# Last ConvFFN of a hybrid decoder step: weights kept over two parts, the last norm without GpSimd, Newton's steps by column

## The chip, the cores and the metric

The kernel runs on one core of a Trainium2 chip. The metric is the time of one execution on the device in microseconds (us). Engines in the profile: PE is TensorE's matrix products, PEld its weight loads, DVE is VectorE, ACT is ScalarE, POOL is GpSimd, SP is SyncE, which issues the DMAs here.

## The reference

One step of a two-layer decoder for a prompt group of 512 tokens and a sample group of 64 (8 sequences of 8 tokens); 576 tokens in all, model width 1024, all in fp32. Layer 0 is attention of two kinds, layer 1 a chunked gMLP. Behind each mixer stands a ConvFFN:

```python
def conv_ffn(h, prev, w_up, w_conv, b_conv, w_down):
    up = h @ w_up                                  # 1024 -> 2 * 2816
    full = jnp.concatenate([prev, up], axis=1)
    y = b_conv
    for k in range(CONV_W):                        # causal, per column, width 3
        y = y + w_conv[k] * full[:, k:k + T]
    gate, val = jnp.split(y, 2, axis=-1)
    return (gelu(gate) * val) @ w_down             # 2816 -> 1024
```

and around each of the four sub-layers `x = layer_norm(ALPHA * x + (1 + gate) * sublayer(h), g, b)`, where `h = x * (1 + scale) + shift` comes from a conditioning vector. The norm takes (x - mean) / sqrt(var + eps), times g, plus b. The last ConvFFN's norm gives the outputs `y_prompt` and `y_sample`.

## The kernel before

Activations lie transposed: 8 blocks of 128 model columns on the partitions, 576 tokens along the free axis. fp32 products are made of three reduced-precision ones: `split_to` (L757) and `weights` (L243) divide a tensor into a high half (a cast on ScalarE) and a low half (a subtraction), and `product` (L287) adds wh*h, wh*l and wl*h over the blocks of a chunk, in PSUM. The tokens come in two parts: part 0 is 0 to 255, part 1 is 256 to 575 (256 prompt tokens and the 64 of the samples). An execution order per engine is made by a planner, from a model of the engines, with the place in the program as priority; `high_priority(offset=n)` shifts that place, `late` ties an instruction behind the one before it on its engine.

`weights` loads a unit of 128 x 1024 by a DMA into a raw buffer, casts it into a high buffer and subtracts into a low one, three buffers of each (`WB`). Which engine subtracts goes by the letters of `lows` in turn: 'g' is GpSimd, 'v' VectorE; in the products that end in a norm it is `LB` = 'gv'.

`ffn` (L471) runs over 22 pairs of hidden blocks. For each it makes the up-projections of gate and value, the convolution (ScalarE and VectorE), the gelu and the split, and it calls the down-projection chunk by chunk (`CH`). The last two chunks, hidden blocks 14 to 17 and 18 to 21, go through `accumulate` (L306) with a norm: part 1 first, through both chunks and all 8 output blocks, then part 0. A unit holds two output blocks of a chunk, so there are four units per chunk and part, and each is loaded and converted for either part: 16 in all. Each block's product goes to `add_gated` (L434), which adds it to the residual on VectorE (L439; part 1 also L442 and L444 for the samples). There are four PSUM buffers for products.

In the second of the two chunks `Norm.collect` (L71) follows every second block: it transposes the residual to rows of tokens (L83, L91), takes statistics on VectorE (L86, L93) and copies the rows on ScalarE (L87, L94). `finish(part)` (L117) calls `moments` (L446): aggregation (L452), then the inverse root in three Newton steps of three small instructions each, on all columns at once (L460 to L462), a column for each 128 tokens: 3 in part 1, 2 in part 0; the gMLP's own norm has 5. For the last norm `prepare` (L96) loads g and b as rows, and `output` (L185) makes the result: for part 1 the normalisation on ScalarE (L195), times g on VectorE (L196), plus b on GpSimd (L197); for part 0 `centre` (L170) has already made (row - mean) * g before Newton's steps, one of its four pieces on VectorE (L180) and three on ScalarE and GpSimd (L182, L183), and one instruction on VectorE remains for each (L199). L200 sends each piece of 512 columns to the output. `finish(1)` stands before part 0's products in the program, and its instructions mix with them.

For the inner norms `finish` normalises the rows (L134, L136), transposes them back (L153) and makes the next stage's modulated input, whose high and low halves are the tiles `xh` and `xl` (made by `pair(xp, [P, KB, T], "x")`, one buffer each), which all up-projections read.

Of the kernel before, what the change touches and what calls it, by code (L numbers as in the profile page):

```python
# [10 lines left out]
F32 = mybir.dt.float32  # L11
# [3 lines left out]
OP = mybir.AluOpType  # L15
# [3 lines left out]
P = 128  # L19
# [30 lines left out]
TWB = 3  # L50
BP = 200
LOWS = 'g'
LA = 'g'
# [6 lines left out]
class Norm:  # L60
# [56 lines left out]
    def finish(self, part):  # L117
# [3 lines left out]
        if last:  # L121
            return self.output(part, r, None)
        shift = self.pool.tile([P, 2 + part], F32, name="shift", bufs=2)
        nc.vector.scalar_tensor_tensor(shift, mv[:, :, 0], -1.0, r, op0=OP.mult, op1=OP.mult)
        if not self.nxt:
            return self.output(part, r, shift)
        t0 = PARTS[part][0]
# [42 lines left out]
    def centre(self, mv):  # L170

        nc, rt = self.net.nc, self.rt
        low = self.pool.tile([P, 2], F32, name="low")
        nc.vector.tensor_scalar(low, mv[:, :, 0], -1.0, None, op0=OP.mult)
        for half in range(2):
            cols = slice(512 * half, 512 * half + 512)
            for i in range(2):
                row, g = rt[:, i, cols], self.gb[:, 0, cols]
                if half == i == 0:
                    nc.vector.scalar_tensor_tensor(row, row, mv[:, i, 0:1], g, op0=OP.subtract, op1=OP.mult)  # L180
                else:
                    nc.scalar.activation(row, row, AF.Identity, bias=low[:, i:i + 1])  # L182
                    nc.gpsimd.tensor_tensor(row, row, g, op=OP.mult)  # L183

    def output(self, part, r, shift):  # L185

        net, nc, rt = self.net, self.net.nc, self.rt
        for half in range(2):
            cols = slice(512 * half, 512 * half + 512)
            for i in range(2 + part):  # L190
# [3 lines left out]
                if part:  # L194
                    nc.scalar.activation(row, row, AF.Identity, bias=shift[:n, i:i + 1], scale=r[:n, i:i + 1])  # L195
                    nc.vector.tensor_tensor(row, row, g, op=OP.mult)  # L196
                    nc.gpsimd.tensor_tensor(row, row, b, op=OP.add)  # L197
                else:
                    nc.vector.scalar_tensor_tensor(row, row, r[:n, i:i + 1], b, op0=OP.mult, op1=OP.add)  # L199
                nc.sync.dma_start(net.a["o_y"][t0:t0 + n, cols], row)  # L200


class Net:
# [102 lines left out]
    def accumulate(self, x, src, chunks, g1, psum, pool, between=None, norm=None):  # L306


        ws = {}

        def step(k0, ops, ob, part):
            m = len(ops)

            n = 1024 // (m * P) if norm else 1
            key = k0, ob // n, part if norm else 0
            if key not in ws:
                cols = slice(k0 * P, (k0 + m) * P)
                unit = src[ob, :, cols] if n == 1 else src[ob:ob + n, :, cols].rearrange("o p k -> p o k")
                ws[key] = self.weights(unit, n * m * P)
            acc = self.product(psum, *ws[key][:2], ob % n * m, ops, part)  # L320
            self.add_gated(x, acc, g1, ob, pool, part)

        if norm is None:
# [6 lines left out]
            return  # L330
        keep, self.lows = self.lows, LB
        for part in (1, 0):
            for k0, ops in chunks:
                for ob in range(8):
                    step(k0, ops, ob, part)
                    if between:
                        between()
                    if k0 == chunks[-1][0]:
                        norm.collect(ob, part)
            if part:  # L340
                norm.prepare()
# [104 lines left out]
    def moments(self, stats, pool, then=None):  # L446
# [12 lines left out]
        for _ in range(3):  # L459
            nc.vector.tensor_mul(z, y, y)  # L460
            nc.vector.tensor_mul(z, z, v)  # L461
            nc.vector.scalar_tensor_tensor(y, z, 1.5, y, op0=OP.add, op1=OP.mult)  # L462
        return mv, y
# [1170 lines left out]
```

## Time and profile before

| | us |
|---|---|
| median of 3 runs | 1940.66 |
| lowest, highest | 1937.17, 1941.69 |
| the profiled execution | 1944.53 |
| its span | 1942.8 |
| mean granted clock of TensorE in it | 0.972 |

The profile is of one execution. The span goes from the first instruction to the end of the last; the rest of the execution's time lies around it. In a row of a timeline stand the start in us from the span's start, the time it took (of several in a row: from the first start to the last end), the engine, the line, the operation, the tiles it writes and reads, their shapes and the count; in square brackets the idle time before it and who ended it. A row of the chain of waits has start, length, engine, tile, line and count. A row of windows has a stretch and its length, then the busy time of PE, PEld, DVE, ACT and POOL with the count of their instructions, the granted clock of TensorE (1.00 is full, 0.50 the lower level), the share of the DMA engines and GB/s; for the instructions of one line alone only the engines that run it are listed. A row of groups has line, engine, operation, tiles, shapes and count, then the busy time, the mean duration of one in ns and the idle time before.

### The profile page before, as it was taken

What the parts mean: (1) busy time and instruction counts of PE and PEld (TensorE: products, weight loads), DVE (VectorE), ACT (ScalarE), POOL (GpSimd) and SP (SyncE); (2) the same over time, 40 slices, a digit from 0 to 9 for tenths busy, and PEclk for the clock granted to TensorE, in tenths of its full rate; (3) what the DMA queues carried; (4) which work ended last, traced back from release to release, by engine and by line L of the source; (5) the groups of instructions that cost most, each with busy time, mean ns of one, the idle gap of its engine ahead of it and who ended that gap; (6) DMA issues with size and microseconds to landing.
All of it is one profiled execution on the core that took longest, in us unless ns stands there. A gap on an engine that the chain in (4) does not pass through costs nothing. (4 is left out here: it accounts for less than half of the span.)

```text
span 1942.8 us, 37068 instructions
## 1 busy us (share of the span) xinstructions
PE 1826.5 (94%) x14460; PEld 1622.8 (84%) x14460; DVE 1157.8 (60%) x2426; ACT 743.7 (38%) x1382; POOL 351.3 (18%) x518
## 2 busy tenths in 40 slices
PE   6889999899889899999999999999998999999996
PEld 4647877655459799999999989999997999999995
DVE  2549963465448754545556963465577655555577
ACT  2323222255443542424345432422234535344543
POOL 2323511110015310101012330110013101010124
PEclk9989999999899999999999999999998999999997
DMA  8346577797874335353543422332132222213242
GB/s 288 127 155 219 179 253 244 241 307 232 266 240 149 116 131 189 135 161 135 195 141 107 131 92 78 97 97 59 63 112 72 78 97 67 97 56 108 87 139 92
DMA packets 140865, 283.36 MB, mean 146 GB/s; under 512 B 32722, under 2 KB 43922, under 8 KB 140690
## 3 DMA queue, kind: packets, MB, share of 16 engines
q1 hardware_dynamic: 139970, 278.64, 43.9%
q0 software_dynamic: 720, 2.36, 0.5%
q8 instruction: 114, 1.87, 0.4%
q14 instruction: 61, 0.50, 0.1%
HBM read 270.00 MB, written 10.94 MB: 145 GB/s over the span
## 5 line engine op out<-in xcount | busy, mean ns | idle before, releaser
L298 PE MATMUL acc<-xl,wh 128*128 128x256 f32 (+1 forms) x1664 | 496.2, 298 | 5.9 <-DVE xl L162 5.9
L298 PE MATMUL acc<-xh,wh 128*128 128x256 f32 (+1 forms) x1664 | 498.6, 300 | 2.9 <-ACT xh L161 1.7
L298 PE MATMUL acc<-xh,wl 128*128 128x256 f32 (+1 forms) x1664 | 495.0, 298 | 0.0
L251 ACT CAST wh<-wr 128x1024 fp32r<-128x1024 f32 (+2 forms) x276 | 260.7, 949 | 537.3 <-PE acc L298 375.3
L254 DVE TENSOR_TENSOR wl<-wr,wh 128x1024 fp32r<-128x1024 f32 (+2 forms) x211 | 226.7, 1076 | 248.0 <-ACT wh L251 222.4
L298 PEld LDWEIGHTS acc<-xh,wh 128*128 128x128 f32 x1664 | 318.2, 191 | 11.7 <-issue 6.4
L298 PEld LDWEIGHTS acc<-xl,wh 128*128 128x128 f32 x1664 | 318.5, 191 | 7.5 <-DVE xl L162 7.1
L298 PEld LDWEIGHTS acc<-xh,wl 128*128 128x128 f32 x1664 | 318.5, 191 | 0.4 <-issue 0.4
L254 POOL TENSOR_TENSOR wl<-wr,wh 128x1024 fp32r<-128x1024 f32 x65 | 160.9, 2476 | 526.6 <-ACT wh L251 471.8
L298 PE MATMUL acc<-gl,wh 128*128 128x256 f32 (+1 forms) x704 | 209.5, 299 | 0.0
L298 PE MATMUL acc<-gh,wl 128*128 128x256 f32 (+1 forms) x704 | 207.8, 298 | 1.6 <-DVE wl L254 1.6
L298 PE MATMUL acc<-gh,wh 128*128 128x256 f32 (+1 forms) x704 | 208.2, 301 | 0.4 <-ACT gh L760 0.4
L439 DVE SCALAR_TENSOR_TENSOR x<-acc,g,x 128x256 f32<-128x256 f32 x256 | 119.7, 476 | 116.9 <-PE acc L298 111.5
L525 DVE SCALAR_TENSOR_TENSOR y<-up,wc,y 128x592 f32<-128x592 f32 x176 | 150.6, 856 | 34.0 <-ACT y L522 30.0
L298 PEld LDWEIGHTS acc<-gh,wh 128*128 128x128 f32 x704 | 132.9, 190 | 5.5 <-ACT wh L251 2.1
L298 PEld LDWEIGHTS acc<-gh,wl 128*128 128x128 f32 x704 | 132.8, 190 | 2.9 <-DVE wl L254 1.9
L298 PEld LDWEIGHTS acc<-gl,wh 128*128 128x128 f32 x704 | 133.9, 190 | 0.3 <-DVE gl L761 0.2
L518 POOL COPY tail<-up 128x2 f32<-128x2 f32 x88 | 26.3, 299 | 519.1 <-ACT up L516 518.8
L516 ACT COPY up<-acc 128x256 f32<-128x256 f32 x176 | 65.2, 371 | 129.9 <-PE acc L298 121.7
L283 PE MATMUL s<-wh,xh 128*128 128x256 f32 (+1 forms) x256 | 81.7, 327 | 1.4 <-ACT wh L251 1.4
L522 ACT ACTIVATE y<-up,wc 128x592 f32<-128x592 f32 x88 | 77.8, 884 | 9.2 <-POOL up L514 1.1
L285 PE MATMUL s<-wh,xl 128*128 128x256 f32 (+1 forms) x256 | 81.3, 317 | 0.0
(442 smaller groups left out, 3468.3 us busy)
## 6 DMA issues: line engine op xcount, KB each, us to landing
wr<-in_w_up SPq DMA_DIRECT2D x88, 512.0 KB
wr<-in_w_down SPq DMA_DIRECT2D x32, 512.0 KB
wh<-in_w_mod SPq DMA_DIRECT2D x30, 512.0 KB
wl<-in_w_mod SPq DMA_DIRECT2D x30, 512.0 KB
wr<-in_w_mod SPq DMA_DIRECT2D x28, 512.0 KB
own<-in_kT_b SPq DMA_DIRECT2D x48, 256.0 KB
own<-in_v_b SPq DMA_DIRECT2D x44, 256.0 KB
wr<-in_w_down SPq DMA_DIRECT2D x32, 320.0 KB
```

The costliest lines, as they stand in the source:

```text
L251: nc.scalar.copy(h, r)
L254: (nc.vector if low == "v" else nc.gpsimd).tensor_sub(l, r, h.bitcast(F32))
L283: mm(out, sh, mh, start=start, stop=False)
L285: mm(out, sl, mh, start=False, stop=stop)
L298: mm(acc, w[:, k * P:(k + 1) * P], m, start=i == 0, stop=i == n - 1)
L439: nc.vector.scalar_tensor_tensor(xp, acc[:, :256], g1[:, ob, 0:1], xp, op0=OP.mult, op1=OP.add)
L516: nc.scalar.copy(u[:, 2 + 256 * part:258 + 256 * part], accs[part][:, :256])
L518: nc.gpsimd.tensor_copy(tail[:, blk, 0:2], u[:, NP:NP + 2])
L522: nc.scalar.activation(y[:, :n], u[:, 0:n], AF.Identity, bias=wc[:, 3, blk:blk + 1], scale=wc[:, 0, blk:blk + 1])
L525: nc.vector.scalar_tensor_tensor(y[:, :n], u[:, k:k + n], wc[:, k, blk:blk + 1], y[:, :n], op0=OP.mult, op1=OP.add)
```

## The change

Four edits, all in the last norm and what feeds it, but for the last:

- In the two last chunks of the last ConvFFN, the high and low halves of the first chunk's weights are written to new tiles in the place of `xh` and `xl` (`stay`) and used for both parts. Of the second chunk, part 1 takes the blocks in the order 6, 7, 0 to 5, so that the units of blocks 0 to 5 are still in the three buffers for part 0; only the unit of blocks 6 and 7 is loaded again. All low halves there are made on VectorE.
- `centre` runs all four pieces on VectorE, and `output` of part 1 is two instructions on VectorE for each piece instead of one on each of ScalarE, VectorE and GpSimd.
- The output of part 1 is given a place 100 further back in the planner's priority (`TL`).
- `moments` with up to three columns makes Newton's steps column by column, two instructions for a column and step, with the column itself as the scalar operand. This holds for all four of the sub-layers' norms.

```diff
--- before.py
+++ after.py
@@ -49,6 +49,7 @@
 LB = 'gv'
 TWB = 3
 BP = 200
+TL = 100
 LOWS = 'g'
 LA = 'g'
 OC = ((0,4),(4,8))
@@ -120,10 +121,11 @@
         mv, r = net.moments(self.stats[:, 2 * part:3 * part + 2], self.pool, self.centre if last else None)
         if last:
             return self.output(part, r, None)
+        if not self.nxt:
+            with net.tc.high_priority(offset=-TL):
+                return self.output(part, r, mv)
         shift = self.pool.tile([P, 2 + part], F32, name="shift", bufs=2)
         nc.vector.scalar_tensor_tensor(shift, mv[:, :, 0], -1.0, r, op0=OP.mult, op1=OP.mult)
-        if not self.nxt:
-            return self.output(part, r, shift)
         t0 = PARTS[part][0]
         for half in range(2):
             cols = slice(512 * half, 512 * half + 512)
@@ -170,19 +172,13 @@
     def centre(self, mv):
 
         nc, rt = self.net.nc, self.rt
-        low = self.pool.tile([P, 2], F32, name="low")
-        nc.vector.tensor_scalar(low, mv[:, :, 0], -1.0, None, op0=OP.mult)
         for half in range(2):
             cols = slice(512 * half, 512 * half + 512)
             for i in range(2):
                 row, g = rt[:, i, cols], self.gb[:, 0, cols]
-                if half == i == 0:
-                    nc.vector.scalar_tensor_tensor(row, row, mv[:, i, 0:1], g, op0=OP.subtract, op1=OP.mult)
-                else:
-                    nc.scalar.activation(row, row, AF.Identity, bias=low[:, i:i + 1])
-                    nc.gpsimd.tensor_tensor(row, row, g, op=OP.mult)
-
-    def output(self, part, r, shift):
+                nc.vector.scalar_tensor_tensor(row, row, mv[:, i, 0:1], g, op0=OP.subtract, op1=OP.mult)
+
+    def output(self, part, r, mv):
 
         net, nc, rt = self.net, self.net.nc, self.rt
         for half in range(2):
@@ -192,11 +188,8 @@
                 t0, n = net.tok(tb)
                 row, g, b = rt[:n, tb, cols], self.gb[:n, 0, cols], self.gb[:n, 1, cols]
                 if part:
-                    nc.scalar.activation(row, row, AF.Identity, bias=shift[:n, i:i + 1], scale=r[:n, i:i + 1])
-                    nc.vector.tensor_tensor(row, row, g, op=OP.mult)
-                    nc.gpsimd.tensor_tensor(row, row, b, op=OP.add)
-                else:
-                    nc.vector.scalar_tensor_tensor(row, row, r[:n, i:i + 1], b, op0=OP.mult, op1=OP.add)
+                    nc.vector.scalar_tensor_tensor(row, row, mv[:n, i, 0:1], g, op0=OP.subtract, op1=OP.mult)
+                nc.vector.scalar_tensor_tensor(row, row, r[:n, i:i + 1], b, op0=OP.mult, op1=OP.add)
                 nc.sync.dma_start(net.a["o_y"][t0:t0 + n, cols], row)
 
 
@@ -308,15 +301,18 @@
 
         ws = {}
 
+        stay = norm and not norm.nxt and [t.rearrange("p k t -> p (k t)") for t in self.pair(pool, [P, KB, T], "x")]
+
         def step(k0, ops, ob, part):
             m = len(ops)
 
             n = 1024 // (m * P) if norm else 1
-            key = k0, ob // n, part if norm else 0
+            key = k0, ob // n, part if norm and not stay else 0
             if key not in ws:
                 cols = slice(k0 * P, (k0 + m) * P)
                 unit = src[ob, :, cols] if n == 1 else src[ob:ob + n, :, cols].rearrange("o p k -> p o k")
-                ws[key] = self.weights(unit, n * m * P)
+                out = [t[:, ob * m * P:(ob + n) * m * P] for t in stay] if stay and k0 == chunks[0][0] else None
+                ws[key] = self.weights(unit, n * m * P, out)
             acc = self.product(psum, *ws[key][:2], ob % n * m, ops, part)
             self.add_gated(x, acc, g1, ob, pool, part)
 
@@ -328,15 +324,19 @@
                     if between:
                         between()
             return
-        keep, self.lows = self.lows, LB
+        keep, self.lows = self.lows, "v" if stay else LB
         for part in (1, 0):
             for k0, ops in chunks:
-                for ob in range(8):
+                final = k0 == chunks[-1][0]
+                for ob in (6, 7, 0, 1, 2, 3, 4, 5) if stay and final and part else range(8):
                     step(k0, ops, ob, part)
                     if between:
                         between()
-                    if k0 == chunks[-1][0]:
+                    if final:
                         norm.collect(ob, part)
+                if stay and final and part:
+
+                    del ws[k0, 3, 0]
             if part:
                 norm.prepare()
             else:
@@ -457,9 +457,17 @@
         nc.vector.tensor_scalar(z, mv[:, :, 1], EPS, None, op0=OP.add)
         nc.vector.tensor_scalar(y.bitcast(I32), z.bitcast(I32), -0.5, float(0x5F3759DF), op0=OP.mult, op1=OP.add)
         for _ in range(3):
-            nc.vector.tensor_mul(z, y, y)
-            nc.vector.tensor_mul(z, z, v)
-            nc.vector.scalar_tensor_tensor(y, z, 1.5, y, op0=OP.add, op1=OP.mult)
+            if n > 3:
+                nc.vector.tensor_mul(z, y, y)
+                nc.vector.tensor_mul(z, z, v)
+                nc.vector.scalar_tensor_tensor(y, z, 1.5, y, op0=OP.add, op1=OP.mult)
+                continue
+
+            cols = [slice(i, i + 1) for i in range(n)]
+            for c in cols:
+                nc.vector.tensor_scalar(z[:, c], y[:, c], y[:, c], v[:, c], op0=OP.mult, op1=OP.mult)
+            for c in cols:
+                nc.vector.tensor_scalar(y[:, c], z[:, c], 1.5, y[:, c], op0=OP.add, op1=OP.mult)
         return mv, y
 
     def tok(self, tb):
```

## Rows read from the trace of the kernel before

**Rows 1.** Windows of all engines over the kernel's last stages, in order.

```profile
1864.06:1894.22 30.16, 30.16 (x212) 29.98 (x211) 27.53 (x62) 11.84 (x16) 10.10 (x4) 1.00 0.51 162
1894.22:1912.53 18.31, 18.31 (x156) 18.07 (x154) 16.12 (x42) 11.38 (x16) 8.80 (x5) 1.00 0.43 129
1912.53:1927.43 14.90, 9.80 (x53) 9.22 (x54) 10.25 (x13) 1.81 (x3) 8.63 (x5) 0.66 0.22 70
1927.43:1942.80 15.37, 1.15 (x9) 0.67 (x7) 10.57 (x25) 3.12 (x5) 3.71 (x3) 0.63 0.19 69
```

**Rows 2.** Timeline of TensorE, where it idles in part 0.

```profile
1915.92 0.48 PE L83 MATMUL tc<-c_ident,x 128*128 128x128 f32 x1 [3.39 <-DVE x L439]
...
1920.71 0.58 PE L298 MATMUL acc<-gh,wl 128*128 128x256 f32 x1 [1.57 <-DVE wl L254]
```

**Rows 3.** Timeline of VectorE, the last norm's gain for part 1.

```profile
1911.20 4.27 DVE L196 TENSOR_TENSOR rt<-rt,gb 128x512 f32<-128x512 f32 x2
```

**Rows 4.** Timeline of GpSimd, bias of part 1 and gain of part 0.

```profile
1908.55 6.38 POOL L197 TENSOR_TENSOR rt<-rt,gb 128x512 f32<-128x512 f32 x4 [4.33 <-DVE rt L196]
...
1931.51 3.71 POOL L183 TENSOR_TENSOR rt<-rt,gb 128x512 f32<-128x512 f32 x3 [9.72 <-ACT rt L182]
```

**Rows 5.** Timeline of VectorE, the last norm of part 0.

```profile
1929.78 0.75 DVE L180 SCALAR_TENSOR_TENSOR rt<-rt,mv,gb 128x512 f32<-128x512 f32 x1
...
1930.52 0.16 DVE L456 TENSOR_SCALAR var<-mv 128x2 f32<-128x2 f32 x1
1930.59 0.16 DVE L457 TENSOR_SCALAR rsz<-mv 128x2 f32<-128x2 f32 x1
1930.79 0.17 DVE L458 TENSOR_SCALAR rsy<-rsz 128x2 int32<-128x2 int32 x1
...
1931.58 1.21 DVE L460 TENSOR_TENSOR rsz<-rsy 128x2 f32<-128x2 f32 x1
...
1935.85 2.74 DVE L199 SCALAR_TENSOR_TENSOR rt<-rt,rsy,gb 128x512 f32<-128x512 f32 x4
```

**Rows 6.** The chain of waits: three transposes, and 34 products of part 0.

```profile
1893.07 0.33 PE tp L83 x3
...
1898.12 4.03 PE acc L298 x34
```

**Rows 7.** Windows of part 0, lines L196 (VectorE) and L254 (VectorE, GpSimd) alone.

```profile
1894.22:1927.43 33.21, 8.62 (x6) 0.85 0.33 103
...
1894.22:1927.43 33.21, 4.68 (x3) 7.62 (x3) 0.85 0.33 103
```

**Rows 8.** Groups of VectorE between 1864.06 and 1894.22 (part 1).

```profile
L444 DVE TENSOR_TENSOR x<-x,gst 128x64 f32<-128x64 f32 x15 | 9.1, 606 | 0.3
...
L254 DVE TENSOR_TENSOR wl<-wr,wh 128x1024 fp32r<-128x1024 f32 x4 | 4.8, 1210 | 0.0
...
L442 DVE TENSOR_TENSOR gst<-acc,g 128x64 f32<-128x64 f32 x15 | 3.1, 210 | 0.0
```

**Rows 9.** Timeline of ScalarE at the end of the last up-projection.

```profile
1864.14 1.05 ACT L251 CAST wh<-wr 128x1024 fp32r<-128x1024 f32 x1 [1.52 <-PE acc L298]
1865.10 0.37 ACT L516 COPY up<-acc 128x256 f32<-128x256 f32 x1
1865.56 0.89 ACT L522 ACTIVATE y<-up,wc 128x592 f32<-128x592 f32 x1
```

**Rows 10.** Two idle times of TensorE elsewhere, in timeline and windows.

```profile
1121.55 0.33 PE L83 MATMUL tc<-c_ident,x 128*128 128x128 f32 x1 [2.10 <-DVE x L439]
...
1122.60:1126.00 3.40, 3.40 (x14) 2.09 (x13) 3.09 (x17) 1.17 (x2) 0.00 (x0) 0.50 0.14 34
...
576.00:584.00 8.00, 6.51 (x44) 6.22 (x43) 3.80 (x15) 1.64 (x2) 4.08 (x3) 1.00 0.95 329
```

**Rows 11.** Timeline behind the gMLP's norm: last normalised rows, first transposes.

```profile
1487.67 1.52 ACT L134 ACTIVATE z<-z,shift,rsy 128x512 f32<-128x512 f32 x2 [3.18 <-DVE shift L124]
...
1492.91 1.03 PE L153 MATMUL tp<-c_ident,z 128*128 128x128 f32 x8
```

## The prediction

> **What bounds the kernel now.** I read four views. First the chain that ended last: outside its last 80 us it is products of TensorE almost without a break, so the change can only win at the end of the kernel, where its parts lie, or lose where it makes TensorE wait. Then the last 80 us cut into stages [rows 1]. The first stage is part 1 of the last two chunks (tokens 256 to 575): 30.16 us, TensorE busy throughout, clock 1.00. Part 0 follows (tokens 0 to 255): 18.31 + 14.90 = 33.21 us, and in its second stretch TensorE is busy for 9.80 of 14.90 us at a mean clock of 0.66. The tail from the last product to the end takes 15.37 us.
>
> Why part 0 breaks off is in the timelines. TensorE idles 3.39 us for a residual addition on VectorE and then 1.57 us for a low half of the weights [rows 2]; after the first of these the clock is at its lower level. That addition stood behind two multiplications by the norm's gain which took 4.27 us together [rows 3], while GpSimd ran its four additions of the norm's bias [rows 4]. Four instructions of nearly the same shape with GpSimd idle take 2.74 us [rows 5], so VectorE works at a third of its pace beside GpSimd.
>
> **Part 0 without its breaks.** The change keeps the low and high weights of both chunks, so part 0 converts one unit of weights instead of eight, and the output of part 1 runs on VectorE alone at a lowered priority. What TensorE has to do stays: 192 products at 4.03/34 = 0.1185 us are 22.75 us, and 18 transposes at 0.11 us are 1.98 us [rows 6], together 24.7 us. If nothing holds it up, 33.21 - 24.7 = 8.5 us go. I take the whole of it, because VectorE then has room: it was busy 16.12 + 10.25 = 26.37 us in part 0 [rows 1]; out go the six gain multiplications (8.62 us) and three low halves (4.68 us) [rows 7], in come twelve scalar_tensor_tensor at 2.74/4 = 0.685 us [rows 5], that is 8.2 us, one low half at 1.2 us [rows 8], and 9 more small instructions of Newton's steps at 0.07 us [rows 5], 0.6 us. That makes 23.1 us, at least 1 us less for what GpSimd stretched among the small ones, inside 24.7 us. The cover is thin: with it gone, VectorE's remainder falls behind the last product and into the tail, about 1 to 2 us. Bounds of the term: -8.5 us, and -4.3 us if half of the holds stay. ScalarE loses seven casts and nine activations, which frees nothing else: its next work waits for VectorE's statistics.
>
> The one unit that is loaded again (blocks 6 and 7) needs a buffer that the first blocks of part 0's second chunk free; from there to its use lie four products' blocks of 12 x 0.1185 us, 5.7 us, against a cast of 0.96 us [rows 9] and a subtraction of 1.2 us. Nothing. On SyncE's queue seven loads of 512 KB go; the six outputs of part 1 stay ahead of the last four, and the reload's raw buffer is free before part 0 begins, so I cost the queue at nothing; if the reload were issued behind outputs that wait for VectorE, those 5.7 us are its cover. GpSimd's queue holds nothing else there.
>
> **The tail.** From the first centring to the first output instruction 1935.85 - 1929.78 = 6.07 us pass [rows 5]. Before, one centring ran on VectorE and three on ScalarE and GpSimd (3.71 us [rows 4]), and three of Newton's small instructions swelled to 1.2 us each meanwhile. After: four centrings at 0.685 us are 2.74 us, three opening instructions 0.47 us. Small instructions start 0.07 us apart when they don't need each other (1930.52, 1930.59) and 0.20 us apart when they do (1930.59, 1930.79) [rows 5]. By columns a step is two pairs, the second of each pair in the shadow of the first: 2 x 0.20 us; three steps 1.2 us in place of 1.8 us. Sum 4.4 us, so -1.7 us. Bounds: 0 (the planner puts part 1's leftovers in between) and -2.3 us (the openings hide between the centrings).
>
> The Trainium skill speaks against the columns: "VectorE: DVE Perf Modes", Terms and Rules for kernel authors, has every VectorE instruction drained before the next one issues, and tells to minimise the count of instructions. By that, twelve instructions would take longer than nine, and the sum would be 1935.8 us (the rival on the count, below). The starts 0.07 us apart contradict it as far as instructions without a common operand go.
>
> **The new wait.** The kept high and low halves of the first chunk lie in the tiles of the modulated input. Those are read until the last product of the up-projection, which ends at the border of the first stage, 1864.06. Before, the first weights of the chunk went to buffers of their own, ahead of that moment, and TensorE went on without a break. Now the cast can't begin until that product is done. At that moment ScalarE also gets the copy of the last up-projected block and the convolution's first activation, earlier in the program: copy to activation 0.46 us, activation 0.89 us, then the cast at 1865.10 - 1864.14 = 0.96 us [rows 9]. 1864.14 + 1.35 + 0.96 gives the first product at 1866.45: **+2.4 us**. If the cast goes first, it is 1.0 us; a gain is excluded, since no other product is left to run. The low half needs VectorE for 1.2 us more, but 16 of the unit's 24 products use only the high half and last 16 x 30.16/212 = 2.3 us [rows 1], so I cost it at nothing; behind two taps of the convolution it may add 1.2 us.
>
> What the clock does after such a gap: an idle of 2.10 us was followed by 3.40 us at 0.50, while 1.49 us of idling in a stretch of 8 us left it at 1.00 [rows 10]. 2.4 us lies on the side of the first, so half of 3.4 us is lost, **+1.7 us**; bounds 0 and, as in part 0 (8.5 us less the two idles of together 4.96 us), 3.6 us.
>
> **VectorE in part 1** now makes all eight low halves, GpSimd none. It was busy 27.53 of 30.16 us there [rows 1]. The small additions to the sample columns took 9.1 us for 15, the multiplications of the same size beside them 3.1 us: some 6 us were GpSimd's doing. Four more low halves add 4 x 1.21 us [rows 8]: 27.5 - 6 + 4.8 = 26.3 us of 30.16 us. Cost nothing, with 3.9 us to spare.
>
> **Newton's steps in the inner norms.** Their transposes stand behind the next stage's first products on TensorE: the last normalised rows were ready at 1487.67 + 1.52 = 1489.2, the transposes began at 1492.91 [rows 11]. So 0.6 us more or less there is hidden by 3.7 us; I take nothing. Bounds: -3.7 us if the planner now puts the transposes earlier, +0.6 us where the cover is short. With five columns the code is as it was.
>
> **Sum.** -8.5 - 1.7 + 2.4 + 1.7 = -6.1 us. The profiled execution took 1944.53 us with a span of 1942.8 us, 3.9 us above the median of the runs; the saving carries over, 1944.53 to 1938.4 us there, and 1940.66 to **1934.6 us** at the median. A change under 0.2% (3.9 us) can't be told from none here.
>
> **Rivals.**
> - *Short gap.* The cast goes first and the clock holds: 1940.66 - 8.5 - 1.7 + 1.0 = 1931.5 us. For it: 1.49 us of idling elsewhere cost no clock. Against it: the copy stands earlier in the program. Earlier transposes in an inner norm come to the same, 0.20 with it.
> - *VectorE still holds part 0.* The twelve instructions of part 1's output are put ahead of additions for which TensorE waits; half of the 8.5 us stays: 1934.6 + 4.3 = 1938.9 us. For it: 22 to 23 us of work in 24.7 us. Against it: the lowered priority, and no single instruction over 1.2 us any more. 0.17.
> - *Count, not columns.* If two instructions on different columns of a tile start 0.20 us apart like dependent ones, twelve take 2.4 us, 1.2 us more than in the forecast, and the tail wins 0.5 us instead of 1.7 us: 1935.8 us. Against it are the starts 0.07 us apart [rows 5], which wrote different tiles. 0.10.
> - *Slower: part 1 becomes VectorE's.* Every unit's low half comes late by the 1.2 us of a subtraction, so TensorE idles 9.6 us in part 1 instead of 2.4 us, and the clock falls with it; in part 0, 5 us of idling cost 3.6 us of clock, so 9.6 us cost about 7 us. 1940.66 - 8.5 - 1.7 + 9.6 + 7 = 1947.1 us. It decides where VectorE's demand in part 1 passes 30.2 us; it stands at 26.3 us. 0.08.
> - That the loads stay would show in their count; the keys of the units leave no way for it.
>
> **How the numbers follow.** The forecast has 0.45, its own range is 1932 to 1937.5. The range of all: down to 1928.5 us, the short gap with some of the 3.7 us of an inner norm; up to 1941 us, a held part 0 with the low half waited for as well. It leaves out the slower rival and the far ends, under 2 in 10. Faster by over 0.2% (below 1936.8): most of the forecast, the short gap, over half of the count rival, 0.66; slower by over 0.2%: 0.08; within: 0.26.
>
> **What would show it.** Nine loads of the second layer's last two chunks instead of sixteen and no GpSimd in the last 80 us; a gap of 1 to 2.5 us on TensorE at the end of the up-projection, its releaser ScalarE's cast; part 0 of 25 to 26 us at clock 1.00; four centrings back to back and Newton's pairs 0.07 us apart; 4.4 us from the first centring to the first output. The forecast is wrong if part 0 keeps an idle of over 2 us, or if part 1 takes over 35 us.

## The result, and the profile after

The changed kernel takes **1925.3 us** (median of 6 runs, 1919.2 to 1929.9) against 1939.5 us for the kernel before beside it: ratio 0.9919 [0.9899, 0.9939], that is 15.7 us less by the ratio (11.8 to 19.6); the medians lie 14.2 us apart. The forecast was 1934.6 us, and its range went down to 1928.5 us. The profiled execution has a span of 1919.2 us, against 1942.8 us.

First the stages on which the forecast spoke: windows over the last stages of the changed kernel, with the columns of [rows 1].

```profile
1848.43:1880.76 32.33, 30.83 (x213) 30.09 (x211) 25.96 (x66) 11.52 (x15) 0.00 (x0) 1.00 0.41 133
1880.76:1905.43 24.67, 24.48 (x209) 24.28 (x208) 22.33 (x63) 3.65 (x7) 0.00 (x0) 1.00 0.16 54
1905.43:1919.18 13.75, 1.25 (x10) 0.77 (x8) 9.68 (x30) 1.45 (x3) 0.00 (x0) 0.67 0.21 77
```

Part 1 takes 32.33 us (30.16 before), part 0 24.67 us (33.21), the tail 13.75 us (15.37): together 8.0 us less. That leaves more than half of the span's 23.6 us to be found elsewhere. Most of it is in the three norms inside the kernel, where the only code that changed is Newton's steps. Each window begins at the first BATCH_NORM_AGGREGATE of a norm's part 1. The second ends where the third begins; the first and the third end at an activation of the convolution behind them, the same one in every kernel. The kernel before, then the changed one.

```profile
616.13:764.96 148.83, 142.78 (x1115) 133.68 (x1114) 94.29 (x178) 64.42 (x108) 29.32 (x54) 0.98 0.42 142
1092.15:1460.84 368.69, 364.96 (x2771) 346.56 (x2770) 214.65 (x460) 121.24 (x192) 52.43 (x39) 1.00 0.28 89
1460.84:1596.16 135.32, 125.74 (x902) 122.24 (x901) 87.54 (x170) 59.80 (x105) 26.63 (x52) 0.95 0.25 81
```

```profile
612.02:757.65 145.63, 141.89 (x1115) 133.70 (x1114) 92.58 (x190) 64.47 (x109) 29.89 (x54) 0.98 0.43 145
1085.10:1448.67 363.57, 362.02 (x2771) 345.49 (x2770) 211.37 (x472) 121.65 (x192) 53.66 (x39) 1.00 0.29 90
1448.67:1580.53 131.86, 124.55 (x902) 122.18 (x901) 86.15 (x182) 60.13 (x105) 25.66 (x52) 0.95 0.26 83
```

The three stages, called A, B and C below, lose 3.2, 5.1 and 3.5 us, **11.8 us** together. TensorE's instructions are the same in number. Its idle time falls by 6.8 us and its busy time by 5.0 us; 2.9 us of the latter lie in B, where a stretch at the lower clock is gone (below). VectorE has twelve instructions more in each stage and is busy for less. The rest lies ahead of the first norm (616.1 against 612.0 us, 4.1 us), less 0.3 us lost between A and B. No experiment has anything to do with the time ahead of the first norm, and it varied between 607.7 and 618.4 us among the profiled executions of this study, so I leave it out. Without it the span gives 19.5 us, at the far end of the interval of the runs. The stages themselves repeat well: A to C together take 652.7 to 653.0 us in four kernels whose inner norms are as before (before, `e2`, `e5`, `e6` below), and 641.1 to 641.7 us in three that have them as changed (after, `e1`, `e9`).

**Where VectorE loses the time.** The timelines of VectorE and of GpSimd at the beginning of stage C, and TensorE's next idle time, in the kernel before:

```profile
1464.13 0.16 DVE L460 TENSOR_TENSOR rsz<-rsy 128x3 f32<-128x3 f32 x1
1464.32 2.25 DVE L461 TENSOR_TENSOR rsz<-rsz,var 128x3 f32<-128x3 f32 x1
...
1467.27 2.24 DVE L461 TENSOR_TENSOR rsz<-rsz,var 128x3 f32<-128x3 f32 x1
...
1464.12 2.43 POOL L254 TENSOR_TENSOR wl<-wr,wh 128x1024 fp32r<-128x1024 f32 x1 [4.68 <-ACT wh L251]
1467.08 2.41 POOL L254 TENSOR_TENSOR wl<-wr,wh 128x1024 fp32r<-128x1024 f32 x1 [0.53 <-ACT wh L251]
...
1471.92 0.46 PE L140 MATMUL tp<-c_ident,z 64*128 64x64 f32 x4 [2.78 <-DVE z L136]
```

A multiplication of three elements per partition takes 2.25 us instead of 0.16 us. It begins just behind the start of a GpSimd subtraction and ends with it (1466.57 against 1466.55). The norm's scaling and TensorE's transposes stand behind it. The group of each line of Newton's steps over the whole kernel (median and longest in ns) says the same, before, and below it after:

```profile
L461 DVE TENSOR_TENSOR rsz<-rsz,var x27: 151/161/2248, 620.1 to 1935.5; 128x3 f32<-128x3 f32 x12, 128x2 f32<-128x2 f32 x12, 128x5 f32<-128x5 f32 x3
```

```profile
L468 DVE TENSOR_SCALAR rsz<-rsy,var x60: 255/265/275, 614.3 to 1912.2; 128x1 f32<-128x1 f32 x60
L470 DVE TENSOR_SCALAR rsy<-rsz,rsy x60: 196/204/213, 614.9 to 1912.5; 128x1 f32<-128x1 f32 x60
```

Before, 8 of the 99 instructions of Newton's steps lasted over 0.5 us (13.0 us together); after, none of 147, though GpSimd works beside them as before: 31 of the 120 column instructions lie wholly inside one of its subtractions. The Trainium skill has the rule, in "SBUF — State Buffer", Who interferes with whom: an instruction of VectorE with two inputs in SBUF contends with a GpSimd instruction that reads SBUF, one with at most one such input outside the modes with two ports doesn't. The trace agrees, 2.25 us with two inputs against at most 0.275 us for the columns; in which mode an instruction ran, no run here shows.

**Where TensorE loses it.** In stage B the first idle time of [rows 10], 2.10 us for a residual addition with 3.40 us of half clock behind it, is gone: the same transpose now waits 0.77 us, and the clock stays at 1.00 from 1105 to 1119 us.

```profile
1109.43 0.33 PE L84 MATMUL tc<-c_ident,x 128*128 128x128 f32 x1 [0.77 <-DVE x L439]
```

### The profile page after: what moved, and what is told of

Read it like the earlier page. It is cut to its first block, busy times and chain, and to the rows that moved or that the text cites. A ratio compares the mean times of both kernels' runs of the same rounds, so it can differ in the third digit from the quotient of the medians.

```text
span 1919.2 us, 37062 instructions
## 1 busy us (share of the span) xinstructions
PE 1818.3 (95%) x14460; PEld 1619.9 (84%) x14460; DVE 1144.1 (60%) x2482; ACT 730.8 (38%) x1366; POOL 318.7 (17%) x501
## 4 chain that ended last, share of the span: by engine, by line
PE 75%; DVE 11%; DMA 3%; ACT 1%; issue 1%; SPq 1%; DVEq 0%; ACTq 0%
PE acc L291 54%; PE s L1337 2%; PE acc L276 2%; PE acc L278 2%; PE acc L277 2%; PE tc L375 1%; PE o L1371 1%; DVE tmp L161 1%; PE o L1290 1%; PE s L276 1%; PE tc L710 1%; PE s L278 1%; PE tp L1281 1%; PE s L277 1%; DMA wr<-in_kT_a 1%
## 5 line engine op out<-in xcount | busy, mean ns | idle before, releaser
L244 ACT CAST wh<-wr 128x1024 fp32r<-128x1024 f32 (+2 forms) x265 | 249.3, 945 | 533.8 <-PE acc L291 368.8
L247 DVE TENSOR_TENSOR wl<-wr,wh 128x1024 fp32r<-128x1024 f32 (+2 forms) x208 | 221.7, 1067 | 248.9 <-ACT wh L244 217.8
L247 POOL TENSOR_TENSOR wl<-wr,wh 128x1024 fp32r<-128x1024 f32 x57 | 141.2, 2477 | 489.0 <-ACT wh L244 470.8
L291 PE MATMUL acc<-gl,wh 128*128 128x256 f32 (+1 forms) x640 | 189.2, 297 | 0.0
L291 PE MATMUL acc<-gh,wh 128*128 128x256 f32 (+1 forms) x640 | 188.3, 299 | 0.4 <-ACT gh L768 0.4
L291 PE MATMUL acc<-gh,wl 128*128 128x256 f32 (+1 forms) x640 | 188.1, 296 | 0.0
L291 PEld LDWEIGHTS acc<-gh,wh 128*128 128x128 f32 x640 | 119.4, 188 | 5.6 <-issue 2.5
L291 PEld LDWEIGHTS acc<-gh,wl 128*128 128x128 f32 x640 | 120.0, 188 | 1.0 <-issue 0.8
L291 PEld LDWEIGHTS acc<-gl,wh 128*128 128x128 f32 x640 | 120.5, 188 | 0.3 <-DVE gl L769 0.2
L526 POOL COPY tail<-up 128x2 f32<-128x2 f32 x88 | 26.3, 299 | 523.4 <-ACT up L524 523.1
```

The costliest lines, as they stand in the source:

```text
L244: nc.scalar.copy(h, r)
L247: (nc.vector if low == "v" else nc.gpsimd).tensor_sub(l, r, h.bitcast(F32))
L291: mm(acc, w[:, k * P:(k + 1) * P], m, start=i == 0, stop=i == n - 1)
L526: nc.gpsimd.tensor_copy(tail[:, blk, 0:2], u[:, NP:NP + 2])
```

## The experiments

The theory after the result: Newton's instructions are held up by GpSimd in their old form, and the residual additions and normalised rows behind them on VectorE are late for TensorE. The rival: the planner, which prices each instruction and sets the order, deals the others around them differently, and the form itself is worth nothing. A third possibility is that the last stages reach back into the stages before.

**The two halves of the change.** `e1_newton_only` is the kernel before with the new steps of `moments`; `e2_rest_only` is the change with the old steps.

```
 e1: before, with the hunk of moments alone       e2: all hunks but that of moments
```

> The kernel before with Newton's steps by column in all norms, nothing else. Theory A (the steps by column change the order of work around the three inner norms and shorten them): 5 to 10 us faster than before, ratio 0.995 to 0.9975; in the profile the three inner norms together are 6 us or more shorter, with the planned order of the changed kernel there. Theory B (the inner norms are not changed by it; the profiled pair differed by chance, above all before 600 us): 0 to 1 us faster, ratio 0.9995 to 1.0. Theory C (by count of instructions): 1 us slower.

> The changed kernel with the old three instructions per Newton step in all norms. Theory A: 6 to 9 us faster than before, ratio 0.9955 to 0.997, all of it behind 1860 us. Theory B: nearly all of the gain, 12 to 15 us, ratio 0.992 to 0.994.

Newton's columns alone: 1927.75 us, 0.9929 [0.9913, 0.9946]. All the rest alone: 1935.25 us, 0.9965 [0.9948, 0.9982]. Stages A to C together take 641.7 us with the columns and 652.7 us without (before 652.8, after 641.1); from the last border on it is 76.3 and 70.4 us (before 78.7, after 70.8). So the two halves are separate, the last stages don't reach back into the stages before, and the half that I had costed at nothing is the larger.

**The two halves of the rest.** `e5_stay_only` takes the kept weights alone, `e6_output_only` the output and the centring on VectorE alone.

```
 e5: before, with the two hunks that name stay    e6: before, with TL and the hunks of centre and output
```

> The kernel before with the kept weights alone (eight low halves of part 1 on VectorE, one reload); the last norm is still spread over ScalarE, VectorE and GpSimd, Newton's steps are the old ones. If the weights are the larger part of the last stages' gain: 4 to 6 us faster than before, ratio 0.997 to 0.998. If GpSimd's additions and products in the norm are: 0 to 2 us faster, with TensorE still idle for over 2 us in part 0. TensorE idles 1 to 2.5 us at the end of the up-projection.

> The kernel before with the last norm's output and centring on VectorE and the lowered priority, old weights (sixteen units, low halves by GpSimd and VectorE in turn), old Newton steps. If the norm's GpSimd work is the larger part of the last stages' gain: 4 to 6 us faster than before, ratio 0.997 to 0.998, no gap at the end of the up-projection. If not: within 2 us of before, because VectorE has four low halves more in part 0 than with kept weights and holds TensorE up.

1935.77 us, 0.9973 [0.9958, 0.9988], and 1936.21 us, 0.9964 [0.995, 0.9979]. Part 0 is 26.4 us with the one and with the other, 24.7 us with both: each alone takes away about 7 of the 8.5 us. `e9_no_stay`, the change less the two hunks that name `stay`, shows what those are still worth beside the rest:

> The changed kernel without the kept weights: sixteen units loaded and converted in the last chunks, low halves by GpSimd and VectorE in turn; output, centring and Newton as changed. If the weights still matter when nothing else of the norm is on GpSimd: the stages behind 1840 us are 2 us or more longer than in the changed kernel, ratio to the kernel before 0.9935 to 0.995. If output and centring already free part 0 and the weights only shift work: within 1 us of the changed kernel, ratio 0.991 to 0.993, with no gap at the end of the up-projection.

1923.34 us, 0.9907 [0.988, 0.9934], which can't be told from the change (0.9919). In its last stages part 1 is back at 30.2 us, without the 2.2 us of waiting, and part 0 is at 26.3 us, the tail at 15.7 us: 72.2 us against 70.8 us.

**Which norm's columns.** `e3_newton_part1` uses the columns for three token blocks only, `e4_newton_part0` for two only:

```
-            if n > 3:
+            if n != 3:        (e3; e4: n != 2)
```

> The kernel before with Newton's steps by column in the norms of part 1 (three columns) alone; part 0 keeps the three wide instructions. If the gain of the inner norms comes from part 1, where VectorE's instructions run beside GpSimd's subtractions: inner norms 9 to 10 us shorter than before together, ratio 0.994 to 0.9955. If it comes from part 0's shorter chain: under 2 us faster. Theory by count: slower by 2 us.

> The kernel before with Newton's steps by column in the norms of part 0 (two columns) alone. Part-1 theory: 1 to 3 us faster, nearly all of it in the tail behind 1927 us, ratio 0.9985 to 0.9995; the three inner norms together within 2 us of before. Part-0 theory: 10 us faster.

1928.87 us, 0.9947 [0.9926, 0.9969], with 641.3 us in A to C; and 1939.68 us, 0.9992 [0.9978, 1.0007], with 653.0 us. All of it is in part 1's norms, those with three blocks.

**Form or order: first try.** `e7_columns_two_tensors` has the columns of `e1`, as scalar_tensor_tensor with a column as second tensor (tensor_scalar reads one tensor and two scalars, scalar_tensor_tensor two tensors and a scalar). `e10_padded` has the old wide steps and more small instructions behind each, whose results nobody uses.

```
-   nc.vector.tensor_scalar(z[:, c], y[:, c], y[:, c], v[:, c], ...)
+   nc.vector.scalar_tensor_tensor(z[:, c], y[:, c], y[:, c], v[:, c], ...)    (e7)
+   for i in range(2 * n - 3 if n < 4 else 0):
+       nc.vector.tensor_scalar(d[:, i:i + 1], v[:, i:i + 1], v[:, i:i + 1], v[:, i:i + 1], ...)    (e10)
```

> The kernel before with Newton's steps by column as in the change, but each of these instructions as a scalar_tensor_tensor, which reads two tensors instead of one tensor and two scalars: the same count, the same results. If the form is what matters (an instruction that reads two tensors waits for GpSimd's running subtraction, one that reads one tensor does not): single instructions of Newton's steps take over 1 us again in part 1, and at most half of the 11.5 us of the three inner norms remain, ratio 0.996 to 0.999. If columns or the order of work matter and not the form: as the run with Newton's steps alone, ratio 0.992 to 0.995.

> The kernel before with the old wide Newton steps and, behind each step, as many small extra instructions on VectorE (on a tile that nobody reads) as the columns would add: three for three columns, one for two. It computes more than the reference asks. If the planner's other order, which longer steps bring, is what saves time in the inner norms: 5 to 10 us faster than before although it does more, ratio 0.995 to 0.9975. If it is the form of the instructions: 0 to 3 us slower than before, ratio 1.0 to 1.0015.

1943.05 us, 0.9998 [0.9984, 1.0011], 653.5 us in A to C; and 1940.03 us, 0.9985 [0.9971, 0.9998], 649.0 us. In the first, 8 of Newton's 147 instructions are held (14.9 us). Its longest, against one for one the same columns in the group shown above:

```profile
L468 DVE SCALAR_TENSOR_TENSOR rsz<-rsy,var x60: 197/212/2462, 619.6 to 1937.2; 128x1 f32<-128x1 f32 x60
```

That shows the form: same shape, same columns, 2.46 us against 0.275 us. But it doesn't settle the time, because the instruction order of the first turned out to be nearly that of the kernel before. Of VectorE's 2345 other instructions in the trace, 7 have to be moved to get from one to the other, against 40 for `e1`. The order of the second is nearer to the new one (17 from `e1`, 37 from before). Form and order had come together.

**Form against order.** Three more kernels part them. In `e13` the form is the old one, and small unused instructions lead the planner to the new order; in `e14` the form is new and the order nearly that of before, at the price of Newton's third step, which it leaves out for three blocks; `e15` is its control with the old form. All change three blocks only, as `e3` does. In the traces `e13` has VectorE's other instructions in the order of `e3` but for one, and from before to `e14` and `e15` 5 and 2 have to be moved. The lines shown stand in place of the three wide instructions of a step, with the ends of the calls left out (`...`).

```
+   for c in cols: nc.vector.scalar_tensor_tensor(z[:, c], y[:, c], y[:, c], v[:, c], ...)        (e13, in each of three steps)
+   for c in cols: nc.vector.scalar_tensor_tensor(y[:, c], z[:, c], 1.5, y[:, c], ...)
+   for i in range(2): nc.vector.tensor_scalar(d[:, i:i + 1], v[:, 0:1], v[:, 0:1], v[:, 0:1], ...)
+   for c in cols: nc.vector.tensor_scalar(z[:, c], y[:, c], y[:, c], v[:, c], ...)               (e14, in each of two steps)
+   for c in cols: nc.vector.tensor_scalar(y[:, c], z[:, c], 1.5, y[:, c], ...)
```

> The kernel before; for three columns Newton's steps go by column with scalar_tensor_tensor (the column as scalar and the column as second tensor), and two small one-tensor instructions behind each step, whose results nobody uses, bring the planner to the order of the kernel with the columns for three tokens blocks alone: all other instructions of VectorE but one stand in its order, those of ScalarE, GpSimd and SyncE all. So the order is that of the run that took 1928.9 us (inner norms 641.3 us), the form that of the kernel before. Theory 'form' (an instruction of two tensors is held while GpSimd works, one of a tensor and scalars is not): the inner norms keep most of their 652.8 us, 648 to 652 us, several of Newton's instructions take over 0.5 us, and the ratio to the kernel before is 0.997 to 1.000. Rival 'order' (only the planner's other order brings the gain, whatever the form): 641 to 643 us, ratio 0.9945 to 0.996.

> The kernel before; for three columns Newton's steps go by column with tensor_scalar, as in the change, but two steps instead of three (the third step is left out, so that the inverse root is less exact): at this count the planner gives nearly the order of the kernel before (10 of VectorE's instructions and 2 of ScalarE's stand elsewhere). So the form is that of the change, the order that of the kernel before. Theory 'form': the inner norms fall from 652.8 us to 643 to 647 us, no instruction of Newton's steps for three columns takes over 0.5 us, ratio 0.994 to 0.9965. Rival 'order': 651 to 653 us (less 0.6 us for each of three left out steps), ratio 0.9985 to 1.000.

> Control of the run with two steps: for three columns two steps by column with scalar_tensor_tensor (the third step is left out) and four small one-tensor instructions ahead of them, whose results nobody uses; the order is that of the kernel before but for 4 instructions of VectorE. Both theories: inner norms 650 to 653 us, ratio 0.998 to 1.000; what it lies below the kernel before is the price of the left out step.

The runs: 1938.34 us, 0.9989 [0.9977, 1.0]; 1940.29 us, 0.9997 [0.9983, 1.0011]; 1941.7 us, 1.0001 [0.9985, 1.0016]. The windows of stages A to C, first `e13`, then `e14`:

```profile
612.08:761.07 148.99, 142.30 (x1115) 133.88 (x1114) 95.17 (x193) 64.51 (x109) 30.14 (x54) 0.98 0.43 142
1088.25:1452.78 364.53, 362.18 (x2772) 345.23 (x2771) 213.84 (x475) 121.77 (x192) 53.84 (x39) 1.00 0.29 90
1452.78:1588.58 135.80, 125.15 (x902) 122.00 (x901) 89.81 (x185) 60.00 (x105) 25.57 (x52) 0.94 0.25 81
```

```profile
618.09:766.07 147.98, 142.62 (x1115) 133.77 (x1114) 93.58 (x181) 64.58 (x108) 29.71 (x54) 0.98 0.43 143
1093.24:1460.82 367.58, 364.20 (x2771) 346.61 (x2770) 213.40 (x462) 121.36 (x192) 52.69 (x39) 1.00 0.29 89
1460.82:1594.13 133.31, 124.96 (x902) 122.04 (x901) 85.64 (x173) 60.00 (x104) 25.68 (x52) 0.95 0.26 83
```

Lengths of the stages (us), from such windows of each kernel:

| order, form | kernel | A | B | C | sum |
|---|---|---|---|---|---|
| old, two tensors | before | 148.8 | 368.7 | 135.3 | 652.8 |
| old, two tensors, two steps | e15 | 149.2 | 368.3 | 135.8 | 653.4 |
| old, one tensor, two steps | e14 | 148.0 | 367.6 | 133.3 | 648.9 |
| new, two tensors | e13 | 149.0 | 364.5 | 135.8 | 649.3 |
| new, one tensor | e3 | 145.5 | 363.6 | 132.1 | 641.3 |

**Neither theory holds alone; both causes are there.** `e13` came out as the theory of the form said, but `e14` didn't: its stages lie between the two theories, and its ratio can't be told from the kernel before. Read by the stages, the order alone wins 3.5 us and all of it in B (4.2 us there): the residual addition before which TensorE idled stands earlier. TensorE's idle time there is 0.75 us in `e13`, and 2.10 us still in `e14`:

```profile
1113.84 0.33 PE L83 MATMUL tc<-c_ident,x 128*128 128x128 f32 x1 [0.75 <-DVE x L439]
```

```profile
1122.21 0.33 PE L83 MATMUL tc<-c_ident,x 128*128 128x128 f32 x1 [2.10 <-DVE x L439]
```

The form alone, in the old order, wins 3.9 us (`e14` against before; 4.5 us against its control), half of it in C, although `shift`, an instruction on two tensors behind Newton's steps, is then held there:

```profile
1467.38 2.10 DVE L124 SCALAR_TENSOR_TENSOR shift<-mv,rsy 128x3 f32<-128x3 f32 x1
```

In the new order the form is worth 8.0 us (`e13` against `e3`), and the runs say the same: 0.9989 [0.9977, 1.0] against 0.9947 [0.9926, 0.9969]. Together form and order win 11.5 us, 4.1 us more than the 3.5 and 3.9 us, and most of what A gains came only with both. In C the new order does nothing for the old form: TensorE's idle times around the norm's transposes are 3.62 + 0.52 + 1.71 us in `e13`, and in `e3`, in the same order with the new form, 0.69 + 2.14 us. TensorE's timelines, with VectorE's and GpSimd's rows of `e3` that answer to the held multiplication shown of before:

```profile
1464.63 0.45 PE L83 MATMUL tc<-c_ident,x 128*128 128x128 f32 x1 [3.62 <-DVE rsz L475]
...
1465.60 0.90 PE L83 MATMUL tc<-c_ident,x 128*128 128x128 f32 x3 [0.52 <-DVE x L439]
...
1468.21 0.68 PE L140 MATMUL tp<-c_ident,z 64*128 64x64 f32 x4 [1.71 <-DVE z L136]
```

```profile
1450.72 0.15 DVE L458 TENSOR_SCALAR rsy<-rsz 128x3 int32<-128x3 int32 x1
1450.91 0.64 DVE L468 TENSOR_SCALAR rsz<-rsy,var 128x1 f32<-128x1 f32 x3
...
1450.90 2.40 POOL L254 TENSOR_TENSOR wl<-wr,wh 128x1024 fp32r<-128x1024 f32 x1 [4.69 <-ACT wh L251]
...
1456.72 0.55 PE L83 MATMUL tc<-c_ident,x 128*128 128x128 f32 x3 [0.69 <-DVE x L439]
...
1459.80 1.09 PE L153 MATMUL tp<-c_ident,z 128*128 128x128 f32 x4 [2.14 <-DVE z L136]
```

Two reservations. `e13` isn't the old form in the new order and nothing else: two of its unused instructions went ahead of the opening of Newton's steps, so that in C it began 3.46 us behind the first aggregation, not 3.10 us as in `e3`. GpSimd's subtraction had then begun (at 3.22 us), and the opening, the same instruction in all kernels, was held for 2.17 us (2.27 us in A). Part of the 8.0 us, some 4 us by the length of these two holds, may thus be the unused instructions' doing, and the order alone may be worth more than 3.5 us; how much, no run here shows. (`e15` has the same two holds, so `e14` is better set against before.) And `e14`'s time fell by less than its stages say (0.6 us, at the most 3.3 us, against 3.9 us). The shares are those of single profiled executions.

**Could more be had?** If GpSimd disturbs VectorE, take GpSimd's work away: `e8_lows_vector` is the change with `LB = 'v'`, all low halves in the products that end in a norm on VectorE. `e11_shift_columns` is the change with the last two-tensor instruction of the norm, `shift`, by column too; `e12_both` has both edits.

```
-LB = 'gv'
+LB = 'v'         (e8)
-        nc.vector.scalar_tensor_tensor(shift, mv[:, :, 0], -1.0, r, ...)          (e11)
+        for i in range(2 + part):
+            nc.vector.tensor_scalar(shift[:, i:i + 1], mv[:, i, 0:1], -1.0, r[:, i:i + 1], ...)
```

> The changed kernel with all low halves in products that end in a norm on VectorE, none on GpSimd (the last norm has that already). If GpSimd's subtractions cost VectorE more by making its two-tensor instructions wait than they save it: the three inner norms shorter by another 3 to 8 us, ratio to the kernel before 0.988 to 0.991. If the eight extra low halves of 1.2 us per norm make VectorE the bound: inner norms longer than in the changed kernel, ratio 0.993 to 0.997.

> The changed kernel with the inner norms' shift (minus mean times inverse root), one instruction on two tensors that took 0.7 to 1.6 us in part 1, made by column too, as one tensor with two scalars. If the form decides: no shift instruction over 0.5 us and the inner norms 1 to 3 us shorter than in the changed kernel, ratio to the kernel before 0.990 to 0.9915. If that wait was hidden or another instruction takes its place: within 1 us of the changed kernel.

> The changed kernel with both of these edits. If they add up: 1 to 3 us faster than the better of the two. With no GpSimd left beside the norm's small instructions the form can no longer matter: then as with the low halves on VectorE alone, within 1 us.

1942.4 us, 1.0001 [0.9986, 1.0016]; 1922.11 us, 0.9901 [0.9877, 0.9926]; 1943.29 us, 1.0006 [0.9991, 1.0022]. GpSimd's share is worth keeping in spite of what it holds up: with VectorE making these low halves, and in the order that the planner then sets, A to C take 659.5 us, 18.5 us more than after, and the whole gain of the change is lost. The shift by column can't be told from the change: none of its instructions takes over 0.21 us, where `shift` took 1.35, 1.60 and 0.68 us in A, B and C after, and yet A to C take 643.4 us, 2.3 us more. A hold that goes isn't time won by itself. With both edits it is as with the first alone.

## Why the prediction was wrong

**The step that failed** is "Newton's steps in the inner norms", which said "I take nothing", with -3.7 us as the far bound. The runs showed -11.5 us (`e3`, stages A to C), -13.8 us in `e1`'s ratio with the last stages. Three things were wrong in it. It judged by [rows 11], a norm of part 0 whose transposes have 3.7 us of cover; `e4` shows that part 0's norms are indeed worth nothing, but in part 1's norms TensorE waits for what stands behind Newton's steps (2.78 us in C before). It costed only the count of instructions; yet [rows 5] shows the sign, a multiplication of two elements at 1.21 us, which I put down to centring in the tail and didn't look for elsewhere. And it took the order of the other instructions nearly as given, though the planner prices every one: 3.5 us or more come from order alone, almost the -3.7 us that it kept for earlier transposes, but in B, where an earlier residual addition brings them. How the 11.5 us divide between form and order stays open.

**Part 0 without its breaks**: right. 24.7 us were forecast, 24.67 us measured, TensorE busy for 24.48 us at clock 1.00; VectorE was busy for 22.33 us, forecast 22 to 23 us. The rival of a held part 0 falls with it. The loads of 512 KB in the last two chunks are nine, before sixteen, and GpSimd does nothing in the last 72 us.

**The tail**: -1.62 us, forecast -1.7 us, but not as forecast. From the first centring to the first output it is 4.84 us, not 4.4 us (6.07 us before), and the other 0.4 us were won behind the first output, where no gain was forecast; that the size came out is partly luck. The timeline of VectorE there:

```profile
1907.78 1.41 DVE L179 SCALAR_TENSOR_TENSOR rt<-rt,mv,gb 128x512 f32<-128x512 f32 x2
...
1910.77 0.46 DVE L468 TENSOR_SCALAR rsz<-rsy,var 128x1 f32<-128x1 f32 x2
1911.14 0.33 DVE L470 TENSOR_SCALAR rsy<-rsz,rsy 128x1 f32<-128x1 f32 x2
1911.39 0.45 DVE L468 TENSOR_SCALAR rsz<-rsy,var 128x1 f32<-128x1 f32 x2
...
1912.62 0.74 DVE L192 SCALAR_TENSOR_TENSOR rt<-rt,rsy,gb 128x512 f32<-128x512 f32 x1
```

A step takes 0.62 us (1910.77 to 1911.39), and the wide ones that nothing holds, in the norm of [rows 11], begin at 1485.65, 1486.23 and 1486.82, 0.59 us apart. So with GpSimd idle the columns win nothing: `e2`, which has the wide steps, has a tail of 13.7 us as well. The rival on the count was right that the columns save nothing, but three steps take 1.9 us, between the forecast's 1.2 us and its own 2.4 us. The rule that the prediction cites from the Trainium skill, to keep the count of instructions low ("VectorE: DVE Perf Modes", Rules for kernel authors), fits the tail by 0.03 us a step; in part 1's norms eighteen instructions beat nine. What the tail wins between centring and output is GpSimd's absence: 4.76 us in `e2` and in `e6`, with the wide steps. In `e9` it is 4.84 us, but the tail is 15.7 us: VectorE was still at the output of part 1 when the last product ended, its last two residual additions came late, and TensorE idled 1.42 us among its last transposes. That is the remainder in the tail which the prediction feared for the change itself.

**The new wait**: its place was right, its size was not. I took 2.4 us and 1.7 us of clock; part 1 grew by 2.17 us, of which 1.56 us lie ahead of the first product. ScalarE and TensorE at the border:

```profile
1848.62 0.38 ACT L524 COPY up<-acc 128x256 f32<-128x256 f32 x1 [2.20 <-PE acc L291]
1848.89 2.94 ACT L244 CAST xh<-wr 128x1024 fp32r<-128x1024 f32 x3
...
1849.99 0.41 PE L291 MATMUL acc<-gh,xh 128*128 128x320 f32 x1 [1.41 <-ACT xh L244]
```

The copy went first, as I had it, but the activation went behind the casts, and the gap is 1.41 us. The clock stayed at 1.00, as after the 1.49 us of [rows 10]: the term of 1.7 us is nothing, as in the rival of the short gap. With VectorE at 25.96 us in part 1 (forecast 26.3 us), the slower rival fell too.

**The sum**: the last stages gave -8.0 us where -6.1 us was forecast, almost all of the difference from the clock; with the inner norms at nothing, that part alone would have been inside the range (`e2`, with the old steps, won 6.8 us by its ratio).

## What to carry to other kernels

Look through VectorE's smallest instructions for long ones: a few that take ten times their median, each ending with an instruction of GpSimd, are time that another form of the same arithmetic can give back. Ask of each what stands behind it on VectorE and whether TensorE waits for that: here the same steps were worth nothing in part 0's norms and 11.5 us in part 1's, with the order that came along. Where a planner sets the order, an edit that is free by its own durations can still move its neighbours; an experiment on the form must say in which order it ran.

## Not expected

- The shield isn't tensor_scalar as such. In `e13` the wide opening of Newton's steps, one tensor and two constants, met a GpSimd subtraction and took 2.17 us, in place of 0.17 us:

```profile
1455.88 0.43 DVE L467 TENSOR_SCALAR pad<-var 128x1 f32<-128x1 f32 x2
1456.24 2.17 DVE L458 TENSOR_SCALAR rsy<-rsz 128x3 int32<-128x3 int32 x1
...
1456.00 2.38 POOL L254 TENSOR_TENSOR wl<-wr,wh 128x1024 fp32r<-128x1024 f32 x1 [4.62 <-ACT wh L251]
```

  The same opening took 2.16 to 2.27 us in A and C of `e10` and `e15`. The single columns of Newton's steps and of `shift`, with scalars from memory, were never held. The Trainium skill ("SBUF — State Buffer", Who interferes with whom) allows for this, since by it tensor_scalar can enter a mode with two ports; which mode the opening ran in, no run here shows.
- Two instructions on different columns of one tile start 0.19 us apart (0.46 us for a pair of 0.27 us each) or 0.13 us (0.33 us for a pair of 0.20 us each), not the 0.07 us of [rows 5], where the two write different tiles.
- One edit, three norms of the same code, three paths: by these single executions it pays mostly by the order in B, mostly by the form in C, and by both together in A.
